# A 20-product algorithm for the second matrix product of a fused two-layer kernel, with running sums put back into PSUM and part of the additions moved to GpSimd

## The chip, the cores and the metric

One core of one Trainium2 chip. The metric is the device time of one execution in microseconds, as the median of several executions. The span of a profile is some 1.7 us shorter than the time of the same run.

## The reference

```python
batch, m, k, h, n = 16, 512, 768, 3072, 768      # x, w1, b1, w2: normal, float32
y = np.maximum(np.matmul(x, w1) + b1, 0)
return np.matmul(y, w2).astype(np.float32)
```

The two products have the same number of multiplications: 8192 x 768 x 3072.

## The kernel before

The hidden width of 3072 is taken in two halves, and the 8192 rows in eight blocks of 1024: 16 passes, counted from 0. The *swap* is the change to the second half of w1 and w2, between passes 7 and 8. In a pass the *first product* makes y, strip by strip (six strips of 2 x 128 hidden columns), and the *second product* multiplies y by w2. Both use Strassen's algorithm on 2 by 2 blocks: seven block products instead of eight. Its operands are sums of blocks in fp16, made in SBUF: for x, for w1, for w2, and for y after each strip. Taking a product's result out of its PSUM bank, with an addition or not, is called its *evacuation*.

```python
def sums_y(self, y):                       # y of one strip: 128 x 7 x 512
    tt = self.nc.vector.tensor_tensor
    tt(out=y[:, self.S1], in0=y[:, self.A21], in1=y[:, self.A22], op=ALU.add)
    a11 = y[:, self.A11:self.A11 + 1].to_broadcast((P, 2, self.MH))
    tt(out=y[:, self.S3:self.S2 + 1:self.S2 - self.S3],
       in0=y[:, self.A21:self.S1 + 1], in1=a11, op=ALU.subtract)
    tt(out=y[:, self.S4], in0=y[:, self.A12], in1=y[:, self.S2], op=ALU.subtract)

def second(self, it, j):                   # one of four row groups of a pass
    ...
    def mm(ps, op, slot, start):           # one product: six matmuls of 384 columns
        for t in range(self.TP):
            nc.tensor.matmul(ps, lhsT=ys[t][:, op, j * P:(j + 1) * P],
                             rhs=ws[t][:, slot, :], start=(start and t == 0),
                             stop=(t == self.TP - 1), skip_group_check=True)
    ...
    return [p1, p2, p6, p5, p7, p3, p4]
```

Every sum of x, w1, w2 and y is on VectorE. The pool of y tiles holds nine strips, so that strips of the next pass are made before the second product of the present one has read its own. The partial results of the first half of the hidden width are fetched from the output ahead of time in the second half, added as the products are evacuated, and stored plainly:

```python
self.y_pool = pool("y", self.TP + 3)
...
for it in range(1, NIT):                   # order of the stages
    if it + 1 < NIT:
        groups += [("m1", it + 1, 0), ("m1", it + 1, 1)]
    groups += [("m2", it, j) for j in range(4)]
    if it + 1 < NIT:
        groups += [("m1", it + 1, t) for t in range(2, TP)]
```

## Time and profile before

| | before |
|---|---|
| time, median (range), us | 899.68 (899.55 to 899.83) |
| matmuls of 384 columns (second product) | 2688 |
| matmuls of 512 columns (first product) | 1890, and 132 (with 24 of 256 columns) in the plain first pass |
| PE busy share | 99% |

The prediction shows the lines that this rests on. I split a span further. From 17.7 us on I take the distance between the starts of successive matmuls and compare it with columns/2.4 plus 2.5 ns, the warm pitch that the trace shows. The sum of these ideal distances is called *work*. What a distance has above it is a *gap* if it is over 0.25 us (0.47 us where the clock record shows half speed), and a *small loss* if it is smaller but over 0.04 us. Small losses are matmuls at half clock and very short waits; in brackets stands the part that lies where the clock record shows half speed. The *rest* is the first 17.7 us and the tail after the start of the last matmul.

| us | span | work | gaps | small losses (at half clock) | rest (of it tail) |
|---|---|---|---|---|---|
| before | 898.0 | 870.5 | 3.6 | 0.2 (0) | 23.7 (5.9) |

### The profile page before, as it was taken

The page shows a single profiled execution, that of the slowest core. Times are in us where ns is not written, and L with a number is a line of the kernel's source. Part 1 is how long each engine was busy: PE and PEld are TensorE (multiplying, and loading weights), DVE is VectorE, ACT ScalarE, POOL GpSimd, SP SyncE. Part 2 cuts the span into 40 slices and gives each one's busy share as a digit, 9 for nine tenths or more (in the row PEclk, how much of TensorE's full clock was granted, in tenths as well). Part 3 has the DMA queues.
Part 4 walks back from the last instruction along what each step waited for, and adds up shares of the span by engine and source line. Part 5 has one row for each costly group of instructions (what it writes and reads, how often), then busy time and mean ns, then how long its engine had stood idle before and what let it go on. Part 6 is the DMA issues. An engine that isn't in the chain of part 4 may idle for free. (4 is left out here: it accounts for less than half of the span.)

```text
span 898.0 us, 13078 instructions
## 1 busy us (share of the span) xinstructions
PE 887.0 (99%) x4805; PEld 472.2 (53%) x4805; DVE 548.5 (61%) x1014; ACT 425.5 (47%) x710; POOL 83.6 (9%) x142
## 2 busy tenths in 40 slices
PE   8999999999999999999999999999999999999997
PEld 6454454554545555454554545545455554545544
DVE  2496746556464664736647666575666757667564
ACT  4757575575756657546444455253503315042220
POOL 6200000000000000012001000101001010010100
PEclk9999999999999999999999999999999999999999
DMA  9979999587595866566759444635445365350613
GB/s 202 200 224 205 341 167 292 108 251 166 125 280 118 266 133 216 201 129 139 191 182 372 162 133 170 216 128 184 156 171 176 137 195 189 114 176 36 211 54 124
DMA packets 106471, 162.52 MB, mean 181 GB/s; under 512 B 67852, under 2 KB 81956, under 8 KB 104356
## 3 DMA queue, kind: packets, MB, share of 16 engines
q1 hardware_dynamic: 67696, 114.44, 36.5%
q0 software_dynamic: 38384, 46.41, 26.2%
q8 instruction: 39, 0.64, 0.3%
q10 hardware_dynamic: 324, 0.80, 0.2%
q14 instruction: 28, 0.23, 0.1%
HBM read 95.37 MB, written 76.48 MB: 191 GB/s over the span
## 5 line engine op out<-in xcount | busy, mean ns | idle before, releaser
L468 PEld LDWEIGHTS <-y 128*128 128x128 f16 x2688 | 263.0, 98 | 187.8 <-issue 2.6
L390 PEld LDWEIGHTS <-w1s 128*128 128x128 f16 x1890 | 184.9, 98 | 212.6 <-issue 1.7
L468 PE MATMUL a<-w2s,y 128*128 128x384 f16 x1536 | 276.4, 326 | 1.9 <-DVE s L473 0.9
L390 PE MATMUL a<-x,w1s 128*128 128x512 f16 x1080 | 267.8, 379 | 0.8 <-DVE y L400 0.8
L396 ACT ACTIVATE s<-a,b1y 128x512 f32<-128x512 f32 x180 | 123.8, 688 | 291.9 <-PE a L390 291.4
L390 PE MATMUL c<-x,w1s 128*128 128x512 f16 x540 | 145.9, 379 | 0.1
L468 PE MATMUL c<-w2s,y 128*128 128x384 f16 x768 | 145.7, 326 | 0.0
L327 DVE TENSOR_TENSOR y<-y 128x512 f16<-128x512 f16 x96 | 40.9, 426 | 119.5 <-ACT y L432 104.0
L473 DVE TENSOR_TENSOR o<-a,s 128x384 f32<-128x384 f32 x64 | 35.6, 556 | 80.4 <-PE a L468 80.3
L400 DVE CUSTOM_DVE_ANT_0 y<-a,s 128x512 f16<-128x512 f32 x90 | 61.7, 685 | 33.1 <-ACT s L396 32.8
L432 ACT ACTIVATE y<-a,b1y 128x512 f16<-128x512 f32 x90 | 61.9, 688 | 33.0 <-PE a L390 33.0
L390 PE MATMUL b<-x,w1s 128*128 128x512 f16 x270 | 73.0, 379 | 0.0
L468 PE MATMUL b<-w2s,y 128*128 128x384 f16 x384 | 72.9, 326 | 0.0
L453 POOL DMA_DIRECT2D o<-out_dram x64 | 34.2, 540 | 389.6 <-DMA out_dram<-o 201.0
L329 DVE TENSOR_TENSOR y<-y 128x1024 f16<-128x1024 f16 x96 | 66.4, 692 | 3.3
L396 ACT ACTIVATE s<-c,b1y 128x512 f32<-128x512 f32 x90 | 61.9, 688 | 8.0 <-PE c L390 8.0
L481 ACT ACTIVATE s<-a 128x384 f32<-128x384 f32 x64 | 31.3, 488 | 71.6 <-PE a L468 70.7
L400 DVE CUSTOM_DVE_ANT_0 y<-b,s 128x512 f16<-128x512 f32 x90 | 61.6, 685 | 2.7 <-PE b L390 1.3
L400 DVE CUSTOM_DVE_ANT_0 y<-c,s 128x512 f16<-128x512 f32 x90 | 61.5, 683 | 0.4
L264 ACT ACTIVATE junk<-xn 128x768 f16<-128x768 f16 x60 | 50.5, 842 | 0.4
L473 DVE TENSOR_TENSOR o<-b,s 128x384 f32<-128x384 f32 x64 | 35.6, 556 | 22.4 <-PE b L468 15.2
L473 DVE TENSOR_TENSOR s<-a,o 128x384 f32<-128x384 f32 x64 | 35.6, 556 | 19.5 <-PE a L468 19.5
(74 smaller groups left out, 425.0 us busy)
## 6 DMA issues: line engine op xcount, KB each, us to landing
out_dram<-o SPq DMA_DIRECT2D x127, 384.0 KB, 3.3
o<-out_dram POOLq DMA_DIRECT2D x64, 384.0 KB, 4.5
xd<-x SPq DMA_DIRECT2D x8, 2688.0 KB, 15.4
x<-xd SPq DMA_DIRECT2D x8, 2688.0 KB, 9.7
xn<-in_x_dram POOLq DMA_DIRECT2D x15, 768.0 KB, 10.7
w1s<-in_w_dram POOLq DMA_DIRECT2D x24, 192.0 KB, 6.5
w2d<-w2t SPq DMA_DIRECT2D x6, 672.0 KB, 8.2
w2s<-w2d SPq DMA_DIRECT2D x6, 672.0 KB, 10.7
```

What stands on the lines that cost most here:

```text
L264: self.nc.scalar.activation(out=junk[:, 0:2].rearrange("p a n -> p (a n)"), in_=rows, func=ACTF.Square, accum_out=self.stat[:, i:i + 1])
L327: tt(out=y[:, self.S1], in0=y[:, self.A21], in1=y[:, self.A22], op=ALU.add)
L329: tt(out=y[:, self.S3:self.S2 + 1:self.S2 - self.S3], in0=y[:, self.A21:self.S1 + 1], in1=a11, op=ALU.subtract)
L390: nc.tensor.matmul(ps, lhsT=w[:, slot, k, :], rhs=x[:, xslot, k, :], start=(start and k == 0), stop=(k == 2), skip_group_check=True)
L396: nc.scalar.activation(out=g[name], in_=ps, func=ACTF.Identity, bias=bias)
L400: nc.vector._custom_dve(TENSOR_ADD_SAT, out=y[:, slot], in0=ps, in1=g[s], s0=F_MAX, s1=0.0)
L432: nc.scalar.activation(out=y[:, self.A21], in_=g["a"], func=ACTF.Relu, bias=bias1)
L453: self.nc.gpsimd.dma_start(out=o[:, half, :], in_=self.rows_of(it, j, half))
L468: nc.tensor.matmul(ps, lhsT=ys[t][:, op, j * P:(j + 1) * P], rhs=ws[t][:, slot, :], start=(start and t == 0), stop=(t == self.TP - 1), ski ...
L473: nc.vector.tensor_tensor(out=o, in0=ps, in1=s, op=ALU.add)
L481: nc.scalar.activation(out=to, in_=ps, func=ACTF.Copy)
```

## The change

The intent: y is now a matrix of 4 by 3 blocks and w2 one of 3 by 2. Plainly that is 24 block products; a list of 20 products does it, so a pass has 160 matmuls of 384 columns where Strassen had 168 (and the plain product 192). More sums are needed. Some running sums of products are therefore written by ScalarE or VectorE back into a PSUM bank, where PE goes on accumulating. All 20 y operands lie in one tile that exists once; U15, which the prediction names, is that of the third product. The 1024 rows of a pass are four *quarters* of 256. To take work from VectorE, half of the y sums (those of quarters 0 and 1, from pass 1 on), all w1 sums and one set of x sums went to GpSimd. Outputs of the second half of the hidden width are added to memory by accumulating DMAs from GpSimd's queue.

The diff runs to over a thousand lines; this is its core.

```diff
-class Strassen:
+class Fast:
+SUMS_Y = (((D101, D104), (A1, A3), (A2, A5), 1), ((U15, D100), (A6, A7), (A8, A8), 1), ...)   # 8 pair sums
+SUMS_W = ((V1, B5, B1, -1), (V15, B0, B1, 1), (B1, B1, B0, -1), ...)                         # 16 sums
+SECOND = (("mm", 16, 1, True), ("mm", 4, 0, True), ("ACT", "s0", 1, 1),
+          ("DVE", "s1", 0, 1, "s0", -1), ("mm", 15, 2, True), ...,
+          ("ACT", "q1", 3, -1), ...)      # q: a pair of PSUM banks, s: SBUF, o: output
-        self.y_pool = pool("y", self.TP + 3)
+        self.y = self.one.tile([P, 20, 4 * self.QM], FP16, name="y")
     def sums_w1(self, w, which=(0, 1, 2, 3)):
-            self.nc.vector.tensor_tensor(...)
+            self.nc.gpsimd.tensor_tensor(...)
-    def sums_y(self, y): ...
+    def sums_y(self, n, s0, s1, engine=None): ...       # pair n, row quarters s0..s1
+    def group_done(self, it, t):                        # after strip t
+        def put(s0, s1, engine):                        # doled out two per step
+            self.fill += [lambda n=n: self.sums_y(n, s0, s1, engine) for n in range(8)]
+        if t == 1:
+            self.sums_y_aside(0, it)
+        elif t == 2:
+            self.sums_y_aside(1, it)
+        elif t == 4:
+            put(2, 3, self.nc.vector)
+        elif t == 5:
+            put(3, 4, self.nc.vector)
+    def sums_y_aside(self, s, it):
+        for n in range(8):
+            self.sums_y(n, s, s + 1, self.nc.gpsimd if it else self.nc.vector)
@@ second
+        def product(p, q, start):
+            for s in range(4):
+                for j in range(2):
+                    m0 = s * QM + j * P
+                    nc.tensor.matmul(self.ps[:, 2 * q + j, 0:NH],
+                                     lhsT=self.y[:, U_OF[p], m0:m0 + P],
+                                     rhs=self.v[:, V_OF[p], s, :], ...)
+                if it < self.NSB:
+                    nc.sync.dma_start(out=rows, in_=o)
+                else:
+                    nc.gpsimd.dma_start(out=rows, in_=o, accum_op=ALU.add)
@@ run
+            groups += [("m1", it, t) for t in range(TP)] + [("m2", it, 0)]
@@ plan: w1 and w2 sums of the start, x sums before the swap of w1 and w2 to the second half
+            put("p1", 0, max(t, 2), 3, lambda t: self.sums_w1(self.w1s[t], (0, 1, 2)), t)
+            put("p1", 0, 4 + n // 8, n % 8 // 2, self.sum_w2, n)
+            put("m2", last, 0, 1, self.sums_x, NSB, n, pool)          # pool: GpSimd
```

## The prediction

> **What bounds the kernel now.** I read the busy shares first, then the line groups, then the timeline of one stretch of second product, and last the timelines of the first 48 and the last 34 us.
>
> Busy shares and slices of the page: only TensorE (PE) is full, in every slice but the first and last.
>
> ```profile
> PE 887.0 (99%) x4805; PEld 472.2 (53%) x4805; DVE 548.5 (61%) x1014; ACT 425.5 (47%) x710; POOL 83.6 (9%) x142
> ...
> PE   8999999999999999999999999999999999999997
> ```
>
> VectorE (DVE) is busy for 61%, ScalarE (ACT) for 47%, GpSimd (POOL) for 9%. So the end is set by how many matmul columns PE streams, and another engine matters only where it makes PE wait. The groups give the durations that I use below (last figures before the bar: mean ns of one).
>
> ```profile
> L390 PE MATMUL a<-x,w1s 128*128 128x512 f16 x1080 | 267.8, 379 | 0.8 <-DVE y L400 0.8
> L468 PE MATMUL a<-w2s,y 128*128 128x384 f16 x1536 | 276.4, 326 | 1.9 <-DVE s L473 0.9
> L327 DVE TENSOR_TENSOR y<-y 128x512 f16<-128x512 f16 x96 | 40.9, 426 | 119.5 <-ACT y L432 104.0
> L473 DVE TENSOR_TENSOR o<-a,s 128x384 f32<-128x384 f32 x64 | 35.6, 556 | 80.4 <-PE a L468 80.3
> L264 ACT ACTIVATE junk<-xn 128x768 f16<-128x768 f16 x60 | 50.5, 842 | 0.4
> ```
>
> The PE mean (326 ns) includes the pipeline, so the pitch has to come from start times. Timeline near the end, first column start in us, second duration:
>
> ```profile
> 868.89 2.11 PE L468 MATMUL a<-w2s,y 128*128 128x384 f16 x12
> ...
> 875.71 2.11 PE L468 MATMUL a<-w2s,y 128*128 128x384 f16 x12
> ...
> 892.49 0.56 DVE L473 TENSOR_TENSOR o<-a,o 128x384 f32<-128x384 f32 x1 [0.42 <-PE a L468]
> ```
>
> Between 868.89 and 875.71 lie one pass of seven products, 42 matmuls: 6.82/42 = 162.4 ns each for 384 columns. In the same way one strip of the first product (21 matmuls of 512 columns) takes 850.99 to 855.52, 215.8 ns each. Pitch is columns/2.4 plus some 2.4 ns, at a granted clock of 1.0. From the first second-product matmul at 43.59 to the last at 892.46 are 848.9 us; the work in it is 2688 x 0.1624 + 1890 x 0.2158 = 436.5 + 407.9 = 844.4, so PE stands for only some 4 us. The tail from the last matmul's end to 898.0 is 5.5 us: one DVE add (0.56), a 192 KB store (2.7) and the program's end.
>
> **What the Trainium skill says.** "TensorE: Matmul & The Clock Gate", section "Wait — 56ns, not 53.3ns?", gives N/2.4 GHz plus about 2.5 ns per warm matmul: this trace agrees (215.8 and 162.4 ns). "GPSIMD Engine Reference", section 3.1, gives about 2.6 cycles of 1.2 GHz per element for a two-input elementwise operation. That makes an estimated 1.1 to 1.2 us for 512 elements; the trace before has no such operation. "SBUF — State Buffer", section "SBUF: two separate sides", says that GpSimd and a VectorE operation with two SBUF inputs take a shared port pair as an exclusive lock for the whole instruction. The trace before can't confirm it, since POOL there issues little but DMAs. "DMA: Bandwidth & Descriptors", section "SWDGE vs HWDGE vs iDMA", says that accumulation during a DMA needs the GpSimd path; its speed isn't given.
>
> **The change part by part.**
>
> *Matmuls.* Each of the 16 passes had 4 x 7 x 6 = 168 matmuls of 384 columns; now 20 products x 8 = 160. The first product keeps its 1890, and the plain first pass its 144. Removed: 16 x 8 x 0.1624 = 20.8 us, all on the critical engine. If PE started and waited as now, it would end at 43.6 + 407.9 + 2560 x 0.1624 = 43.6 + 407.9 + 415.7 = 867.2 us. This sum holds no waits at all, so the 4 us of now are removed in it too, and what follows is added.
>
> *Evacuation.* A pass now has 16 DVE operations and 8 ACT operations of 768 columns. DVE: 556 ns at 384 and 685 at 512 is about 1.04 ns a column, so 556 + 384 x 1.04 = 0.96 us, 15.3 us of a pass of 26 us. ACT: 488 ns for 384, at 0.83 ns a column some 0.81 us, 6.5 us a pass. The y sums stay 32 pair operations of 512 elements a pass: 16 on DVE (16 x 0.426 = 6.8 us), 16 on POOL. DVE per iteration: 12.3 (first product) + 6.8 + 15.3 + 3.6 (x sums) = 38 of 53.2 us. It fits, but order matters, because a product now needs two PSUM banks that were read just before, and often adds to what ACT or DVE has put back.
>
> I walked the order of one pass with these durations, 0.20 us from a product's last column to its reader (as 874.74 to 874.94 in the timeline), and 1.30 us per product. T is the end of the last first-product matmul. The relu ends at T + 0.9; the product with A10 needs it for its last quarter at T + 0.98. The product with U15 needs a DVE sum at T + 2.3, and that is ready at about T + 1.6. The refill of the bank pair q2 waits for an ACT copy that ends at T + 3.6, against T + 3.9. The later steps have 0 to 0.2 us to spare. The eight squares on ACT, 0.83 us apart, fit between. Cost: about 0.15 us a pass, 2 us in all. The order looks tuned.
>
> *Start of the second product.* Here I expect the largest wait. The w2 sums are now 15 DVE operations of 1536 elements in fp16 (0.95 us, as the x sums of that size), and the first needs the last w2 load. In the trace before those loads are issued from 16.8 to 29.1 us and take 7.7 to land, so the last lands at 36.8. From there DVE has 15 x 0.95 with y sums between them in its queue. The y sum of the last quarter that the third product (U15) needs comes after 14 w2 sums and 10 y sums: 36.8 + 14 x 0.95 + 10 x 0.43 = 54.4 us. PE would be there at 43.6 + 2 x 1.30 + 0.98 = 47.2. Wait: 7.2 us, once. Little of this exists before (0.32 us at 46.84).
>
> *Swap of w2 between the halves and x sums on POOL.* Sixteen w2 sums lie in one pass and the next strip stage; DVE there is near 25 of 27 us. I allow 2 us, and 2 more for accumulating DMAs that hold one of four output tiles too long.
>
> *Tail.* The last product is followed by a DVE operation (0.2 + 0.96) and an accumulating DMA of 384 KB from POOL with three more just ahead of it. A POOL load of that size lands in 4.5 us; I take 6. With 2.2 for the program's end that is 9.4 instead of 5.5.
>
> Sum: 867.2 + 2 + 7.2 + 4 + 9.4 = 889.8 of span; the timed run is 1.7 above the span now (899.7 against 898.0), so 891. As I rounded most waits up, I say 889.
>
> **The rivals.**
> (a) *PE pays nothing but the columns.* With the w2 loads earlier and the tail unchanged: 867.2 + 2 + 5.5 + 1.7 = 876. For it: PE is at 99% now, DVE and ACT have room. Against: the queue of w2 sums. With waits of up to 5 us it is still faster by over 2% (under 881.7).
> (b) *POOL and DVE block each other.* POOL's 16 sums begin after strip 1 and 2 of 6. At 1.2 us each they end about T + 2, while DVE's own two-input y sums run from T - 3.9 to T + 9. If each waits for the other's whole instruction, five POOL operations of 1.2 us push into DVE's queue before the sum that U15 needs: about 3.8 us of PE wait a pass, 15 x 3.8 = 57 us, for 945. Against: the sums for these quarters were placed early as if to avoid this, and it vanishes if a POOL sum takes under about 0.85 us. All sums on DVE would by the same walk cost 1 us a pass; nobody would choose POOL if it cost more. I give the full effect one chance in eight, a part of it (5 to 15 us) one in four.
> (c) *Accumulating DMAs are slow.* If 384 KB takes 10 us instead of 6, DVE waits for an output tile in eight passes, for 2 to 3 us, and PE for 1 to 2 of it: 8 to 16 us, near 900.
>
> **Range and chances.** The main line is 889; (a) reaches down to 878, the partial (b) or (c) up to 905, both 915. So 878 to 912 for 8 in 10. Under 881.7: 0.18. Above 917.7, only by (b) in full: 0.12. Within 2%: 0.70.
>
> **What would show it.** Right, if the profile after has 2560 second-product matmuls at 162 ns pitch; one PE gap of 5 to 9 us near 47 us, ended by a DVE y sum; POOL sums of 1.0 to 1.3 us; PE gaps under 0.5 us in the steady passes; and 8 to 10 us from PE's end to the span's end. Wrong by (b), if DVE y sums wait where POOL is busy and the U15 product stands for microseconds in each pass; by (c), if DVE's output operations wait on DMAs in the second half alone; by (a), if there is no gap near 47 us. A granted clock under 1.0 would make all of it void.

## The result, and the profile after

| | before | after |
|---|---|---|
| time, median (range), us | 899.68 (899.55 to 899.83) | 975.11 (972.3 to 976.38) |
| granted clock, runs of one call | 0.998 to 1.0 | 0.961 to 0.971 |

Slower by 8.3%: the ratio is 1.0834, with a 95% interval of 1.0809 to 1.0859. Ratios here and below are the mean time of one kernel's fast runs over the mean of the other's fast runs of the same rounds, so not quite the ratio of the medians quoted. The prediction was wrong in size and in sign.

The split of the span, as above:

| us | span | work | gaps | small losses (at half clock) | rest (of it tail) |
|---|---|---|---|---|---|
| before | 898.0 | 870.5 | 3.6 | 0.2 (0) | 23.7 (5.9) |
| after | 974.7 | 849.9 | 70.4 | 21.2 (18.4) | 33.2 (15.1) |
| difference | +76.7 | -20.6 | +66.8 | +21.0 (+18.4) | +9.5 (+9.2) |

The saving is there, 20.6 us against 20.8 predicted. It is lost three times over in gaps, nearly once more at a halved TensorE clock (18.4 us), and almost half of it again in the tail. The page of the kernel after; busy shares first, then 40 slices of the span in tenths:

```profile
PE 891.1 (91%) x4677; PEld 463.7 (48%) x4677; DVE 653.2 (67%) x866; ACT 485.1 (50%) x731; POOL 472.8 (49%) x433
...
PE   8839989898998999999499999999989899999993
...
PEclk9969999999999999999799999999999999999997
```

PE is no longer full: the third slice (49 to 73 us, the start of the second product) is at three tenths, the twentieth (463 to 487 us, the swap) at four, several others at eight, and the last at three, where it was at seven. Its clock dips in the third, the twentieth and the last slice. POOL went from 9% to 49% of the span. The groups of the same page:

```profile
L596 PE MATMUL ps<-v,y 128*128 128x384 f16 x2560 | 441.5, 334 | 32.7 <-DVE y L458 21.2
L537 PE MATMUL ps<-x,w1s 128*128 128x512 f16 x1890 | 423.6, 381 | 32.8 <-DVE y L549 31.4
L458 POOL TENSOR_TENSOR y<-y 128x512 f16<-128x512 f16 x240 | 280.6, 1189 | 245.9 <-DVE y L549 171.9
...
L549 DVE CUSTOM_DVE_ANT_0 y<-ps,s 128x512 f16<-128x512 f32 x270 | 175.8, 686 | 158.5 <-ACT s L545 117.2
...
L458 DVE TENSOR_TENSOR y<-y 128x512 f16<-128x512 f16 x272 | 185.6, 709 | 16.6 <-ACT y L494 10.4
```

Two numbers matter. A y sum of 128x512 on VectorE now takes 709 ns, against 426 ns for the same shape before. The mean hides two kinds: 169 of the 272 run while GpSimd makes no addition and take 418 ns, the 103 that overlap one take 1187. The evacuation that reads one PSUM operand (L549) takes 686 ns, as its like did before (685). And PE waits for VectorE: 31.4 us for L549 at the first product, 21.2 us for L458 at the second. A timeline of the end of the first product in one pass shows how the two belong together (start, duration, engine, ..., count, idle time before it and what ended that):

```profile
230.62 9.47 POOL L458 TENSOR_TENSOR y<-y 128x512 f16<-128x512 f16 x8
...
234.53 5.85 DVE L458 TENSOR_TENSOR y<-y 128x512 f16<-128x512 f16 x4
...
237.23 0.81 PE L537 MATMUL ps<-x,w1s 128*128 128x512 f16 x3
...
240.29 0.68 DVE L549 CUSTOM_DVE_ANT_0 y<-ps,s 128x512 f16<-128x512 f32 x1
...
241.03 1.38 PE L537 MATMUL ps<-x,w1s 128*128 128x512 f16 x3 [2.99 <-DVE y L549]
```

While POOL works through its eight sums, four sums of VectorE take 5.85 us instead of four times 0.426, 1.7 us: each ends 0.3 us after one of POOL's does. Next in VectorE's queue is the evacuation at 240.29, which is not long itself. It frees the PSUM bank that PE needs for the last product of the strip, so PE stands for 3 us. PE waits 16 times for L549, 31.4 us in all, at most 3.2 at once; no wait of PE, VectorE or ScalarE is ended by a sum of GpSimd. And when PE has stood for 3 us, its clock is halved for a while, as two stretches with the granted clock (column PEclk) show, one after this gap, one after a gap of 1.6 us that begins with the matmul of 411.52:

```profile
core 0: us, PE busy (x) PEld busy (x) DVE busy (x) ACT busy (x) POOL busy (x), PEclk, DMA share, GB/s
...
241.10:244.50 3.40, 3.40 (x11) 1.45 (x11) 2.66 (x7) 2.05 (x4) 2.03 (x3) 0.50 0.92 121
...
413.00:416.40 3.40, 3.08 (x17) 1.50 (x16) 3.33 (x8) 2.21 (x4) 2.33 (x3) 1.00 0.35 32
```

All 11 gaps of 2.33 us and more in this trace end in, or just before, a stretch of 3.4 to 10.2 us at half clock; none of the gaps of 1.6 us and less is followed by one. At the start the same happens for longer, since GpSimd makes the 24 w1 sums there:

```profile
32.05 30.39 POOL L285 TENSOR_TENSOR w1s<-w1s 128x384 f16<-128x384 f16 x24
39.49 9.57 DVE L329 TENSOR_TENSOR v<-v 128x1536 f16<-128x1536 f16 x6
...
52.79 4.41 PE L596 MATMUL ps<-v,y 128*128 128x384 f16 x14 [6.94 <-DVE v L329]
...
67.50 2.74 PE L596 MATMUL ps<-v,y 128*128 128x384 f16 x8 [10.30 <-DVE y L458]
```

Six w2 sums (named v) take 9.57 us, 1.6 each; one of this shape takes 0.95 us in e2 below, where nothing runs on GpSimd beside it. GpSimd waits too: its w1 sums take 1.5 to 1.6 us each beside the w2 sums, and 0.9 to 1.1 at the other times of this stretch. At the swap of the weights a single x sum of 6.04 us on GpSimd stands in front of VectorE's y sums, three of which take 10.12 us:

```profile
468.31 10.12 DVE L458 TENSOR_TENSOR y<-y 128x512 f16<-128x512 f16 x3
...
472.11 6.04 POOL L385 TENSOR_TENSOR x<-x 128x3072 f16<-128x3072 f16 x1
...
482.38 2.10 PE L596 MATMUL ps<-v,y 128*128 128x384 f16 x6 [10.86 <-DVE y L458]
```

By place, the gaps are 19.7 us at the start, 11.0 at the swap, and 39.7 elsewhere. The tail:

```profile
962.66 0.95 DVE L618 TENSOR_TENSOR o<-s,ps 128x768 f32<-128x768 f32 x1 [1.91 <-DMA out_dram<-o]
963.92 1.20 POOL L627 DMA_DIRECT2D out_dram<-o  x1 [1.65 <-DVEq L824]
```

The last output is ready at 963.6 and its DMA leaves GpSimd's queue at 965.1; the span ends at 974.7.

### The profile page after: what moved, and what is told of

It reads as the page before. It is cut to its first block, busy times and chain, and to the rows that moved or that the text cites. A ratio compares the mean times of both kernels' runs of the same rounds, so it can differ in the third digit from the quotient of the medians.

```text
span 974.7 us, 12785 instructions
## 1 busy us (share of the span) xinstructions
PE 891.1 (91%) x4677; PEld 463.7 (48%) x4677; DVE 653.2 (67%) x866; ACT 485.1 (50%) x731; POOL 472.8 (49%) x433
## 4 chain that ended last, share of the span: by engine, by line
PE 67%; DVE 14%; issue 9%; POOL 5%; ACT 2%; DMA 1%; DVEq 0%; POOLq 0%; ACTq 0%
PE ps L596 35%; PE ps L537 31%; DVE y L458 9%; POOL y L458 4%; DVE y L549 3%; DVE v L329 2%; POOL out_dram L627 1%; ACT y L579 1%; DMA out_dram<-o 1%; DMA w1s<-in_w_dram 1%; PE ps L489 1%; ACT s L545 1%; ACT scrap L373 0%; ACT y L494 0%; DVE x L430 0%
## 5 line engine op out<-in xcount | busy, mean ns | idle before, releaser
L596 PE MATMUL ps<-v,y 128*128 128x384 f16 x2560 | 441.5, 334 | 32.7 <-DVE y L458 21.2
L537 PE MATMUL ps<-x,w1s 128*128 128x512 f16 x1890 | 423.6, 381 | 32.8 <-DVE y L549 31.4
L458 POOL TENSOR_TENSOR y<-y 128x512 f16<-128x512 f16 x240 | 280.6, 1189 | 245.9 <-DVE y L549 171.9
L549 DVE CUSTOM_DVE_ANT_0 y<-ps,s 128x512 f16<-128x512 f32 x270 | 175.8, 686 | 158.5 <-ACT s L545 117.2
L545 ACT ACTIVATE s<-ps,b1y 128x512 f32<-128x512 f32 x270 | 179.5, 686 | 199.0 <-PE ps L537 184.5
L458 DVE TENSOR_TENSOR y<-y 128x512 f16<-128x512 f16 x272 | 185.6, 709 | 16.6 <-ACT y L494 10.4
L627 POOL DMA_DIRECT2D out_dram<-o x64 | 77.4, 1263 | 172.0 <-DVE o L618 169.8
L612 ACT ACTIVATE s<-ps 128x768 f32<-128x768 f32 x96 | 77.7, 810 | 143.9 <-PE ps L596 128.7
L618 DVE TENSOR_TENSOR s<-ps,s 128x768 f32<-128x768 f32 x96 | 90.1, 952 | 24.4 <-ACT s L612 11.6
L579 ACT ACTIVATE y<-ps,b1y 128x512 f16<-128x512 f32 x90 | 61.8, 687 | 75.2 <-PE ps L537 75.0
L612 ACT ACTIVATE ps<-ps 128x768 f32<-128x768 f32 x32 | 25.5, 798 | 10.2 <-PE ps L596 10.2
L489 PE MATMUL ps<-x,w1s 128*128 128x512 f16 x132 | 28.8, 379 | 0.4 <-DVE x L430 0.2
```

The source lines that it names most:

```text
L458: (engine or self.nc.vector).tensor_tensor(out=pair(*outs), in0=pair(*ins0), in1=pair(*ins1), op=ALU.add if sign > 0 else ALU.subtract)
L537: nc.tensor.matmul(ps, lhsT=w[:, slot, k, :], rhs=x[:, xslot, k, :], start=(start and k == 0), stop=(k == 2), skip_group_check=True)
L545: nc.scalar.activation(out=kept(name), in_=ps, func=ACTF.Identity, bias=bias)
L549: nc.vector._custom_dve(TENSOR_ADD_SAT, out=self.y_of(self.TP * half + t, m), in0=self.two(ps), in1=self.two(kept(name)), s0=F_MAX, s1=0.0)
L579: nc.scalar.activation(out=self.y_of(t, 1), in_=self.two(g["a"]), func=ACTF.Relu, bias=bias1)
L596: nc.tensor.matmul(self.ps[:, 2 * q + j, 0:NH], lhsT=self.y[:, U_OF[p], m0:m0 + P], rhs=self.v[:, V_OF[p], s, :], start=(start and s == 0) ...
```

## The experiments

**The theories.** *Lock:* GpSimd's sums and VectorE's sums with two SBUF inputs exclude each other, whoever needs the results; everything else (bank late, PE waits, clock) follows. *Late data:* GpSimd is simply slow, and PE or VectorE waits for the results of its sums. *Order:* the new algorithm's own queue on VectorE is too long or in a bad order, wherever the other sums run.

**e1: all y sums on VectorE.** w1 and x sums stay on GpSimd.

```diff
         if t in (1, 2):
-            self.sums_y_aside(t - 1, it)              # GpSimd for it > 0
+            put(t - 1, t, self.nc.vector)             # doled out one per step
```

> The y sums of quarters 0 and 1, which GpSimd makes in every pass after the first, go to VectorE, one after each step of the first product. GpSimd keeps the w1 sums and the x sums of the swap. Theory L (GpSimd's and VectorE's two-input operations hold each other up): VectorE's y sums fall to 0.43 us in the steady passes, the PE gaps of 1.6 to 3.4 us before the last strip product vanish (40 us in all) with the clock drops after them (about 11 us), while the gaps near 46 to 67 us and at 471 us stay: 975 - 51 = 924 us. Theory P (PE waits because GpSimd's sums come late as data): the same gaps vanish, so this run alone doesn't tell the two apart. Theory D (VectorE simply has too much work): sixteen more sums on it make it slower than 975 us.

Measured: 936.60 us (935.28 to 938.91), ratio to before 1.0405 [1.0388, 1.0423]; 38.5 us less than the change. Gaps 44.4, small losses 10.3. The steady gaps before the last product of a strip are gone; the start, the swap and gaps of together some 1.4 to 3 us in each of the passes 1 to 6, where GpSimd makes w1 sums for the second half, stay. The time is 12 us above what I expected, because I had taken the share of those places too small.

**e2: no sums at all on GpSimd.** e1, and w1 and x sums on VectorE too. Some were also placed later in the queue, which the cut shows for the x sums alone: the fourth w1 sum of each strip went into the second product of pass 0, and the w1 sums made ahead of time went further back in their pass.

```diff
     def sums_w1(self, w, which=(0, 1, 2, 3)):
-            self.nc.gpsimd.tensor_tensor(...)
+            self.nc.vector.tensor_tensor(...)
-            put("m2", last, 0, 1, self.sums_x, NSB, n, pool)
+            put("m2", last, 0, 8 + 2 * n, self.sums_x, NSB, n)
```

> As e1, and the w1 sums and the three x sums of the swap go to VectorE too: GpSimd does no two-input operation at all. Theory L: w2 sums on VectorE fall from 1.43 to 0.95 us, the gap at 57 us (10.5 us) shrinks to below 2, the gap at 471 us (11 us) to below 4, with their clock drops: about 895 us. Theory P gives the same for the start only if VectorE had to wait for the w1 sums, which it never did: about 924. Theory D: slower than e1.

Measured: 911.26 us (908.23 to 912.13), ratio 1.0117 [1.0099, 1.0136]; 63.9 us less than the change, though VectorE has more to do. Its group of y sums:

```profile
L458 DVE TENSOR_TENSOR y<-y 128x512 f16<-128x512 f16 x512 | 203.8, 419 | 38.6 <-ACT y L580 23.7 <-ACT y L495 10.4
```

512 sums take 203.8 us in all; in the kernel after, 272 of them took 185.6. But it is 16 us above the expected 895, and slower than before. Gaps 22.1, small losses 6.5, tail 14.0: something else of the change costs too. One wait is by far the largest, in the timeline of the start:

```profile
56.06 3.38 PE L597 MATMUL ps<-v,y 128*128 128x384 f16 x10 [6.68 <-DVE y L458]
```

**e3: GpSimd does the same additions, on a tile of its own that nobody reads** (the true sums are left out, so the result is wrong). **e4: the same, with twice as many fills of that tile instead of additions**, which write and don't read.

```diff
     def sums_y_aside(self, s, it):
         for n in range(8):
-            self.sums_y(n, s, s + 1, self.nc.gpsimd if it else self.nc.vector)
+            if not it: self.sums_y(n, s, s + 1, self.nc.vector)
+            else:                                     # first: one element of y is copied, as a start signal
+                self.nc.gpsimd.tensor_tensor(out=self.decoy, in0=self.decoy, in1=self.decoy, op=ALU.add)  # e3
+                for _ in range(2): self.nc.gpsimd.memset(self.decoy, 0.0)                                 # e4
```

> Wrong result on purpose: in every pass after the first GpSimd makes its 16 two-input sums of 512 elements at the same place in its queue, started by the same relu, but on a tile of its own that nobody reads; the true sums of quarters 0 and 1 aren't made at all. VectorE's and PE's queues are as in the changed kernel. Theory L: the PE gaps of 1.6 to 3.4 us stay, VectorE's y sums beside GpSimd's still take over 1 us, 970 to 980 us. Theory P: nobody waits for GpSimd's data now, so the gaps go and the time is about 924.

> Wrong result on purpose: as e3, but each decoy sum is replaced by two memsets of 512 fp16 elements on GpSimd (about 0.5 us each by the before profile's memsets), which write and don't read. The skill's SBUF page says a VectorE operation with two SBUF inputs is held up only against a GpSimd operation that reads SBUF: then about 924 us with y sums of 0.43 us. If writing alone holds VectorE up too: 960 to 980 us.

Measured, one run each: 972.3 us and 935.97 us. The y sums on VectorE and the stand-ins on GpSimd, first for e3:

```profile
L460 DVE TENSOR_TENSOR y<-y 128x512 f16<-128x512 f16 x272 | 182.8, 697 | 19.3 <-ACT y L505 10.4 <-ACT y L590 7.0
...
L487 POOL TENSOR_TENSOR decoy<-decoy 128x512 f16<-128x512 f16 x240 | 258.0, 1075 | 19.0
```

and for e4:

```profile
L460 DVE TENSOR_TENSOR y<-y 128x512 f16<-128x512 f16 x272 | 125.3, 486 | 24.4 <-ACT y L589 12.1 <-ACT y L504 10.4
...
L488 POOL MEMSET decoy<- 128x512 f16 x480 | 252.1, 525 | 27.6
```

With additions that nobody waits for the time is that of the change, and VectorE's sums are as long (697 against 709 ns). This settles against late data for the y sums; for the w1 and x sums the trace after does, where no wait is ended by a GpSimd sum. The equal time is in part chance: e3 has more gaps (76.4 us against 70.4) and less half clock (8.9 against 18.4), since a pass mostly stands twice, for at most 1.8 us before the strip's last product and mostly 0.9 us in the second product. With as much GpSimd time in fills (252 against 258 us) VectorE's sums take 486 ns, as in e1 (482), and the whole kernel about as long (935.97 against 936.60). What is left above 418 ns comes from the w1 and x sums, which are additions still: the 160 y sums with only fills beside them take 418 ns. So it is not a busy GpSimd that costs, but one that makes additions. They differ from fills by reading SBUF; each fill is also half as long, which this run does not separate. I had expected 924 for e4 by the same mistake as in e1.

**e8: the kernel before, with e3's stand-in additions.** Does the lock by itself do it, or only in the new order?

```diff
             self.sums_y(y)                            # end of a strip, kernel before
+            if t in (1, 2):
+                for n in range(8):                    # first: one element of y is copied
+                    nc.gpsimd.tensor_tensor(out=self.decoy, in0=self.decoy, in1=self.decoy, op=ALU.add)
```

> The kernel before, with the same number of two-input fp16 additions on GpSimd as the change put there for y (16 per pass of 128x512, each reading and writing a tile that nobody else reads; they start when strips 1 and 2 of a pass are done, beside VectorE's y sums of the next strips). Tells whether the lock hurts by itself or only in the changed kernel's order. Theory (GpSimd's reads block VectorE's SBUF-only sums in any kernel; what it costs depends on whether TensorE waits for those sums at once): VectorE's y sums go from 426 ns to some 550 to 650 ns on average, while the time stays under 905 us, for the kernel before holds y twice and makes the sums of each strip long before they are read. Rival (GpSimd work costs the same wherever it stands): 940 us and more.

Measured: 922.93 us (922.7 to 923.49), ratio 1.026 [1.0243, 1.0277]. Both expectations missed: it costs 23.3 us, where I had said about 5 at most, or 40 and more. The first sums of 128x512 went from 426 to 590 and those of 128x1024 from 692 to 812 ns. The first line shows one group, the second what PE waited for longest (us, times, longest):

```profile
L329 DVE TENSOR_TENSOR y<-y 128x512 f16<-128x512 f16 x96 | 56.6, 590 | 99.8 <-ACT y L434 84.3 <-ACT y L347 15.5
...
PE a L392 <- DVE y L402: 19.3, 18, 1.8
```

In the kernel before, PE waited there for 0.8 us in all. L402 is the evacuation of the first product: it queues behind the lengthened sums, and its bank comes free late, by some 1.07 us a pass. That y exists ahead of time there does not help against it, because what comes late is the bank and not y. It is the same chain in a kernel with the old algorithm. Its gaps stay under 2 us, and its record shows no half clock before the tail; in the kernel after the gap of a pass is one and a half to three times as long, and half clock takes 18.4.

**e5, e6: e2 with VectorE's queue put in another order.** e5 loads and sums w2 in the order of need; e6 also spreads the w1 sums of passes 1 to 6 and the w2 sums of the swap.

```diff
-        for s in range(4):                            # e5
-            for q in range(3):
+        for q in (0, 2, 1):
+            for s in range(4):
                 self.load_w2(self.v[:, 2 * q:2 * q + 2], 0, q, s)
-            put("p1", 0, 4 + n // 8, n % 8 // 2, self.sum_w2, n)
+            # nine of the 16 w2 sums in strips 4 and 5, the others one by one in the second product;
+            # w1 sums before them, the fourth of each strip later
-        elif step == 1:                               # e6
-            self.sums_w1(w)
+        elif step < 5:
+            self.sums_w1(w, (step - 1,))
```

> The run with all sums on VectorE (911.26 us) with its start put in another order: w2 loaded quarter by quarter in the order of need, its sums made just ahead of the products that read them, w1 sums earlier. In that run 11.2 us of gaps and most of 6.5 us at half clock stood at the start. Theory (what is left after the lock is gone is a queue of VectorE work at the start that the order of the sums sets): start gaps 1 to 2 us, clock loss about 1 us, 897 us. Rival (TensorE's loss at the start comes from the loads of w2, which the order doesn't shorten): 907 to 911 us.

> The run before it in this list, with the sums for the second half of the columns of w1 spread one per step over passes 1 to 6, and the w2 sums at the swap spread over the first pass of the second half. These places hold 6 gaps of 0.8 us and about 4 us at the swap. Theory of the VectorE queue: 5 to 8 us less than the run before it, about 890 us. Rival (the gaps are PSUM banks that come free late, whatever stands in VectorE's queue): no change over 1 us.

Measured: 906.48 us (905.87 to 906.87), ratio 1.0073 [1.0057, 1.009], and 900.28 us (900.23 to 901.91), ratio 1.0013 [0.9996, 1.0029]. e5 gained 4.8 instead of 14: start gaps of 4.2 and 2.28 us were left, both ended by w2 sums, one on VectorE and one on ScalarE. The order was better but not yet right, which e10 takes up; that the loads bind is not excluded by this run. e6 gained 6.2 more, within the expected 5 to 8: the passes 1 to 6 and the swap were a matter of the queue.

**e7, e9: the tail.** e7 is e6 with eight output tiles in the last pass instead of four. e9 is e6 with the partial results of the last four outputs fetched ahead in the last pass, folded into the sums that these outputs are made from, and stored plainly from SP's queue.

```diff
-            o = self.o_pool.tile([P, 2, NH], FP32, name="o")          # e7
+            o = new_o()                       # last pass: four more, from the pool of raw tiles
+            fold(nc.vector, "s1", "o7", ALU.subtract)                 # e9: kept sum -= partial result
+            fold(nc.vector, "s3", "o1", ALU.subtract)
+            fold(nc.vector, "s5", "o4", ALU.add)
+            fold(nc.gpsimd, "s4", "o6", ALU.add)
-                nc.gpsimd.dma_start(out=rows, in_=o, accum_op=ALU.add)
+                nc.sync.dma_start(out=rows_of(to), in_=o)             # these four
```

> The run before it with eight instead of four output tiles in the last pass. The tail from the last matmul to the end is 14 us in all versions with accumulating DMA, 5.7 us before the change. Theory: part of it is VectorE waiting for an output tile whose accumulating DMA has not landed: tail about 10 us, 3 us less than the run before it. Rival: the tail is the chain of the last sums and the last DMA alone, and stays at 14 us.

> The run with the swap spread (e6, 900.28 us; last matmul starts at 884.55, tail 14.2 us) with another end: in the last pass the partial results of the last four outputs are fetched ahead and folded into the kept sums that these outputs are made from (three on VectorE, one on GpSimd), and stored plainly instead of by accumulating DMA. Theory (the tail is the queue of accumulating DMAs behind the last outputs: four issues of 1.2 us one after another on GpSimd's queue and 7.8 us to land): the four stores leave at once and move 1.5 MB at about 200 GB/s from 884 on: the tail falls to 8 or 9 us, time about 894.5. Rival (the tail is the last sums on VectorE and a DMA's latency whatever its kind): no change over 1 us.

Measured: e7 900.21 us (899.0 to 900.9), ratio 1.0001 [0.9985, 1.0018]: no gain over e6, tail 13.9 us. VectorE's wait for an output tile was real (0.74 and 1.91 us in the kernel after) but not what ended last. e9 896.26 us (895.28 to 897.35), ratio 0.9958 [0.9942, 0.9975]: 4.0 less than e6, tail 10.0 instead of 14.2. It was run on another chip. So about half of what the tail had grown by (5.9 us before) was the queue of accumulating DMAs; I had hoped for 8 to 9. The run changes the kind of store and its queue together and does not tell them apart.

**e10: e9 and the start reordered once more.** The seven w2 sums that the first two products need come first, the w1 sums of strips 3 to 5 after the start, x sums of the first pass a little later.

```diff
-        for n, at in ((0, ("p1", 0, 4, 0)), (1, ("p1", 0, 4, 1)), (2, ("p1", 0, 4, 1)),
-                      (9, ("p1", 0, 4, 2)), (7, ("p1", 0, 4, 2)), (3, ("p1", 0, 4, 2)), ...
+        for n, at in ((0, ("p1", 0, 3, 2)), (1, ("p1", 0, 3, 2)), (2, ("p1", 0, 3, 3)),
+                      (3, ("p1", 0, 4, 0)), (4, ("p1", 0, 4, 1)), (5, ("p1", 0, 4, 2)),
+                      (6, ("p1", 0, 4, 3)), (9, ("m2", 0, 0, 1)), (7, ("m2", 0, 0, 3)), ...
```

> e9 and the start reordered once more: the seven w2 sums that the first two products need come before the y sums of the last quarters, w1 sums of strips 2 to 5 after them, x sums of the first pass a little later. e6 has gaps of 4.2 us and 2.28 us and some 4 us at half clock in the start, and 1.75 us after the swap. Theory (all of that is the order of VectorE's queue): start gaps under 1.5 us and no half clock: 6 to 9 us less than e9, about 887 us, 1.4 per cent faster than the kernel before. Rival (VectorE has too much to do in the start in any order; the loss moves to the next place): 891 us or more.

Measured: 889.25 us (888.63 to 889.39), ratio 0.9882 [0.9865, 0.9898]. It was run on another chip. It is 7.0 less than e9, correct, 1.2% faster than the kernel before and 8.8% faster than the change (889.25/975.11). It fell between my expectation (887) and the rival's (891): of the start, gaps of 1.23, 0.41 and 1.78 us are left, and no half clock before the tail. The page, busy shares and slices:

```profile
PE 869.4 (98%) x4677; PEld 458.1 (52%) x4677; DVE 670.0 (75%) x1160; ACT 485.0 (55%) x731; POOL 123.1 (14%) x139
...
PE   8999999999999999999999999999999999999995
...
PEclk9999999999999999999999999999999999999998
```

VectorE is at 75%, more than in the kernel after (67%), and PE is full. That the start was a matter of order is shown by this run, against e5's rival. The end of it, where the four plain stores leave SP's queue:

```profile
878.04 3.78 SPq L643 DMA_DIRECT2D out_dram<-part  x4
879.66 0.94 DVE L639 TENSOR_TENSOR part<-s,ps 128x768 f32<-128x768 f32 x1
```

The last output is ready at 880.6 and the span ends at 887.6, 7 us later; after the change it was 11 us.

**e11: e10 with the y sums of quarters 0 and 1 back on GpSimd**, as in the change.

```diff
-            put(t - 1, t, self.nc.vector)
+            self.sums_y_aside(t - 1, it)              # GpSimd for it > 0
```

> e10 (889.25 us) with one thing of the change put back: the y sums of quarters 0 and 1 on GpSimd from the second pass on; w1 sums and x sums stay on VectorE, start, swap and end stay reordered. It tells what the y sums alone cost in the steady passes. Theory: in the changed kernel the passes stand 1.6 to 3.4 us before the last strip's product and lose 1 to 2 us to a halved clock after the longer gaps, and taking these sums off GpSimd saved 38.5 us there; so 925 to 930 here, with gaps of 1.6 to 3.4 us per pass before a product that waits for VectorE. Rival (the costs don't add; with the rest of the lock's work gone the sums of y hide): under 905.

Measured: 933.77 us (932.93 to 934.37), ratio 1.0377 [1.0359, 1.0396]: 44.5 us more than e10, and some 4 above what I expected. Gaps rose by 35.2 us and small losses by 9.2, all of it at half clock, together 44.4. The longest wait of PE in it is the one of the kernel after (31.4 us, 16 times) again:

```profile
PE ps L535 <- DVE y L547: 30.5, 16, 3.2
```

So this one part of the change, 16 sums a pass, costs more than twice what the algorithm saves, also where everything else is in order.

The split of the span for the runs that it decides on (e3 and e4 with stand-ins, wrong results):

| us | span | work | gaps | small losses (at half clock) | rest (of it tail) |
|---|---|---|---|---|---|
| after | 974.7 | 849.9 | 70.4 | 21.2 (18.4) | 33.2 (15.1) |
| e3, additions nobody reads | 970.8 | 849.9 | 76.4 | 11.4 (8.9) | 33.1 (15.0) |
| e4, fills | 934.4 | 849.9 | 43.9 | 8.5 (6.0) | 32.1 (14.2) |
| e1, y sums on VectorE | 937.3 | 849.9 | 44.4 | 10.3 (7.8) | 32.7 (14.5) |
| e2, no GpSimd sums | 910.6 | 849.9 | 22.1 | 6.5 (4.2) | 32.1 (14.0) |
| e6, order | 898.7 | 849.9 | 11.6 | 5.1 (2.8) | 32.1 (14.2) |
| e9, tail | 895.6 | 849.9 | 12.6 | 5.1 (2.6) | 28.0 (10.0) |
| e10, start again | 887.6 | 849.9 | 7.4 | 3.0 (0) | 27.3 (9.4) |
| e11, y sums back | 932.5 | 849.9 | 42.6 | 12.2 (9.2) | 27.8 (9.8) |

## Why the prediction was wrong

**Matmuls: right.** 2560 at the old pitch, 20.6 us less work against 20.8.

**Evacuation, durations: right.** VectorE 0.95 us (0.96 predicted), ScalarE 0.81 (0.81), GpSimd's sum 1.19 (1.1 to 1.2). The figures a column that it used, 1.04 and 0.83 ns, don't follow from the lines it shows (VectorE's give 1.01); from 384 to the 768 columns of the kernel after they are 1.03 and 0.84, so the guess held. *The walk of one pass* ("about 0.15 us a pass") can be held only against a kernel without GpSimd sums: e10 has 4.0 us of gaps after the start and 3.0 of small losses, some 0.5 us a pass. The same walk gave 1 us a pass for all sums on VectorE.

**The step that failed: the overlap of GpSimd's and VectorE's sums, entered at no cost.** The main line lets both run side by side; what that costs stood only in rival (b). It measured 44.5 us in e11, about 3 a pass, and 38.5 between the change and e1. The working had the lock from the skill, its direction, and a size of 57 us; then it set that aside with "nobody would choose POOL if it cost more" and "the sums for these quarters were placed early as if to avoid this", and put it at one in eight. Those are guesses at what somebody meant, not readings of a profile. The Trainium skill's page "Perfetto Trace Analysis", section "Optimizing Scalar/DVE Operations", even warns that moving operations between these two engines might not help, as they share a port; I had not weighed it. The walk's own numbers, POOL's sums ending "about T + 2" and VectorE's running "from T - 3.9", already had them side by side for 6 us in every pass. e3 shows that the time stays at 972.3 us when nobody reads the results of GpSimd's y sums, and e11 what these sums cost by themselves.

**Where (b) itself was off.** It had PE stand at "the sum that U15 needs", 3.8 us a pass. The trace has the stand one stage earlier, at the last product of a first-product strip, for want of a PSUM bank: 1.6 to 3.4 us a pass. The lengthened sums push back what stands behind them in VectorE's queue, and what is needed first is the evacuation. Why the early passes wait 3.2 us and the later ones mostly 1.6, I did not settle; e11 has the same pattern, so GpSimd's w1 sums are not the reason. The trace shows a difference: in passes 1 to 4 GpSimd issues a load of w2 (0.72 us) among its sums, and VectorE's four sums before the evacuation are then all lengthened, the first to 2.0 to 2.6 us; where the wait is 1.6 us they take 0.7, 0.7, 1.4 and 1.4. That the load is the cause was not tested.

**Terms missing from the sum.** GpSimd's w1 sums beside the w2 sums at the start: with them PE stands for 19.7 us in the start, without them (e2, which also put six of these sums later) for 11.2. GpSimd's x sums at the swap: 11.0 us against "I allow 2 us" (e2, where VectorE makes them: 5.1 in five gaps between 459 and 492 us). Half clock after the gaps: 18.4 us, which the prediction only had as a general reservation about the clock.

**The start.** "Wait: 7.2 us, once", ended by the y sum for the third product, due at 54.4 us. The kernel after has a gap of 7.1 us near 45.5, which looks like a hit and is not one: it stands before the second product and a w2 sum ends it, lengthened by the lock. The predicted wait is the next one, 10.5 us from 57.0 to 67.5: it stands before the last quarter of the third product, and a y sum ends it, as foreseen. In e2, where nothing is locked, it is 6.85 us at the same matmul, ended at 56. So the place and the kind were right; the time at which the sum is ready was too early by 13 us in the kernel after and 1.6 us in e2, and the wait before the second product was missing.

**The tail.** 9.4 us predicted, 15.1 from the start of the last matmul measured. An accumulating DMA lands in a median of 6.1 us, near the 6 that I took; the four at the end queue: 1.2 us each to issue, one behind the other, and 7.8 us to landing in e7. Rival (c), VectorE waiting for output tiles, is in the trace (28.0 us in 25 waits after the change) and costs PE next to nothing: in e10 VectorE waits 22.3 us for them while all gaps of PE are 7.4 us, and more tiles at the end gained nothing (e7).

**What became of the 889.** e10 runs at 889.25 us. That is the number predicted, and no proof of the working: its tail of 9.4 us is reached by other stores and its start by another order of sums than in the kernel that was predicted. What it does show is that the algorithm is worth 1.2% here, and that the loss of 8.3% lies in where the additions run, in their order, and in the last stores.

## What to carry to other kernels

Before two-input additions go from VectorE to GpSimd, ask whether VectorE has additions of two SBUF operands at the same time: if so, expect both to be lengthened, as here, and everything queued behind them to come late; here the PSUM banks counted first. Moving work off an engine that is 61% busy bought nothing here; VectorE was better off with all of it, at 75%. A longer gap on PE can have a second price, the halved clock after it: in the traces of all runs here 17 of the 21 gaps of 2.28 to 3.4 us that began at full clock were followed by a stretch at half clock, and none of the shorter ones. So a delay that would be bearable at 1 us may not be at 3.

## What the Trainium skill lacked or had wrong

- "SBUF — State Buffer", section "SBUF: two separate sides": the lock is confirmed, its exception too. VectorE's two-input fp16 sum of 128x512 takes 419 ns with no sums on GpSimd (e2), 697 beside GpSimd additions (e3), 486 beside GpSimd fills of the same total time (e4; e1, without them, has 482). Evacuations with one PSUM operand, which the page does not list among the locked ones, kept their 685 ns (686 after). The page lacks what it costs a kernel: 16 additions a pass raised it from 889.25 to 933.77 us (e11).
- "TensorE: Matmul & The Clock Gate", section "Why this matters for your kernels", advises no idle gaps over about 3 us. That is too lenient: gaps of 2.33 us at 593.55 and 651.25 us in the kernel after were each followed by 3.4 us at a granted clock of 0.5. It is not certain either: a gap of 3.38 us in e11 (at 101.08) was not followed by one, and of the 2.28 us gaps at about 71 us those of e5 and e7 were, that of e6 was not.
- "GPSIMD Engine Reference", section 3.1, measures its 2.6 cycles per element in fp32 only. In fp16 128x512 took means of 1.08 (e3) to 1.19 us (after), near the 1.11 us that one estimates from it; the one fp32 sum that GpSimd makes in e10, 128x768, took 2.15 us, more than the 1.66 us so estimated.
- "DMA: Bandwidth & Descriptors", section "SWDGE vs HWDGE vs iDMA", gives no speed for accumulating DMAs. Here 384 KB landed in 6.1 us (median of 64), took 1.26 us of GpSimd's queue to issue, and 7.8 us to landing where four followed each other.
